# Turns by way of DRAM, one ring of eight weight buffers, and pauses counted in matmul time, in a two-layer mLSTM and RG-LRU trunk

## The chip, the cores and the metric

The kernel runs on one core of a Trainium2 chip. The metric is the device time of one execution in microseconds (us). A core has a matrix engine (PE, with its weight loads PEld), a vector engine (DVE), a scalar engine (ACT), GpSimd (POOL) and SyncE (SP, which only issues transfers), and 16 DMA engines that all queues share. Each engine runs its own list of instructions strictly in order; an instruction that waits holds up everything behind it on that engine.

## The reference

Two layers work on x (256 tokens by 2048 channels, float32); a final RMSNorm follows.

```
u = rms_norm(x, norm_g);  p = u @ w_in             # 12304 columns: q,k | v | o | z_a | gates | xb | z_b
q, k = silu(causal_dwconv(qk))                     # 4 taps, along the tokens
h = mlstm_chunkwise(q, k, v, i, log_f)             # 8 heads of matrix memory
y_a = head_norm(h * sigmoid(o)) * head_norm_g * silu(z_a)
xc = causal_dwconv(xb) + b
r, i = sigmoid(xc @ w_a + b_a), sigmoid(xc @ w_x + b_x)       # per head, 256 by 256
y_b = scan(a = exp(-8 r softplus(-lam)), xc * i * sqrt(1 - a*a)) * silu(z_b)
x = x + concat(y_a, y_b) @ w_out
```

## The kernel before, in words

**Products.** Every product is float32 made of three fp32r products: a weight is split into wH (a cast on ACT) and wL = w - wH (a subtraction on DVE), the activations likewise, and PE multiplies high by high, high by low and low by high. A "half" is the unit of work: 512 KB of weights (128 partitions by 1024 floats), its cast, its subtraction and 12 matmuls of 512 columns (24 shorter ones in a gate's half). `mm_a` (L392) keeps the tokens as rows of the result, `mm_b` (L412) the channels.

**Order.** `_sequence` (L45) writes out the order of the halves: per layer four groups of two heads and 512 channels, and in each group the columns for q/k, o, v, xb, z, z_b, the gates, and the 4 output chunks of the group before. Some products are made blockwise with seven instead of eight block products (`block_halves`, L1185): their weights are sums of blocks, which POOL makes ahead of time in DRAM tensors `w_d` with accumulating transfers (`weight_sums`, L1133), and each of their 84 pieces is a "block half" of 6 matmuls, set in between the others.

**The loop** (L1490) walks through the halves. Ahead of half n it loads (on SP), and prepares (wH, wL) halves up to three ahead (AHEAD, L28), for which there are four buffers (`wsp`, L125). Plain halves load into a ring of six buffers (`raw`, tag of the pool `wraw`, L123), block halves into two of their own (`rawb`, `wblk`, L124), with a rule for how far ahead of its place a block half is loaded (BLOCKS_AHEAD, L36 and L1495). Halves of q/k, xb and z_b are "paired": their 512 KB come from two units, in two transfers of 256 KB (L344).

**Work beside.** Everything else (convolution, gates, mLSTM) is written as generators that `pump` (L284) advances between the halves; a `yield "wait"` lets one pass go by, and `st["t"]` counts the matmul time laid down so far (2.72 us a half, 1.36 us a block half, L1520). `qk_post` (L706) makes the scores of the first head (`ps_S`, L752), pauses one pass (L762), makes those of the second, pauses three passes, and multiplies by v (`ps_n`, L675 to L677) for each head. The three auxiliary PSUM banks turn round among these, so the second head's second bank is free only when DVE has read the first head's first one (`Pt`, L758). What the builder lays down is then put into each engine's list by a scheduler of the language; it may move instructions of one engine past each other as long as data and ordering edges hold.

**Turns.** What needs channels as rows is turned: ACT writes `tok`, DVE transposes 32 by 32 blocks into `blk` (L528), and 16 transfers of 32 KB inside SBUF bring the blocks to their partitions, `fr` (L532): 8 from SP, 8 from POOL, and all 16 from SP for the last one, whose `back` is SP (L934). There are 35 turns. Readers of `fr` are `joined` (`ch`, L556), `split_channels` (`tok`, L548) and the z_b step (`zsg` and `zb`, L950 and L951). They are laid down LANDING = 10 us or FAR = 15 us of matmul time after the turn.

**The end.** The last item (`last_out`, L1325) has 16 halves: kp = 0 and 1 (four column chunks each) multiply y_a, kp = 2 and 3 multiply y_b for both token halves. The weights of kp = 2 are cast into buffers of their own, `w_own` (L1430), ordered behind the casts of y_b (`ybH`, `ybL`; L957 and L385); those of kp = 3 use the four `wsp` buffers, which the four halves of kp = 1 hold until PE has used them.

**Pace of the sums.** `weight_sums` keeps an account `st["dma"]` of transfer time: loads add COPY, accumulating transfers ADDING, turns TURN, and each half takes off its time times RATE (L1523). A sum is begun when the account is low, and each begins behind the cast then being made (`paced`, L276).

Of the kernel before, what the change touches and what calls it, by code (L numbers as in the profile page):

```python
# [9 lines left out]
F32 = mybir.dt.float32  # L10
# [6 lines left out]
P = 128  # L17
# [5 lines left out]
NG = 4  # L23
# [6 lines left out]
FAR = 15.0  # L30
BORDER = 7
BLANKS = 7
RATE = 0.9, 0.75
COPY, ADDING, TURN = 1.3, 2.6, 1.7
SUMS_FROM = 20
BLOCKS_AHEAD = 5  # L36
FULL = 3.0
LAG = {"wH": 0, "wL": 1}

# [60 lines left out]
def tile_trunk(ctx, tc, x, xt, par, gw, gb, ws, final_g, out):  # L100
    nc = tc.nc
    G, PE = nc.gpsimd, nc.tensor
# [17 lines left out]
    V, S = Behind(nc.vector, "wL"), Behind(nc.scalar, "wH")  # L120

    const = ctx.enter_context(tc.tile_pool(name="const", bufs=1))
    wraw = ctx.enter_context(tc.tile_pool(name="wraw", bufs=6))  # L123
    wblk = ctx.enter_context(tc.tile_pool(name="wblk", bufs=2))  # L124
    wsp = ctx.enter_context(tc.tile_pool(name="wsp", bufs=4))  # L125
    act = ctx.enter_context(tc.tile_pool(name="act", bufs=1))
    work = ctx.enter_context(tc.tile_pool(name="work", bufs=1))
# [1 line left out]
    dram = ctx.enter_context(tc.tile_pool(name="dram", bufs=1, space=bass.MemoryType.DRAM))  # L129
# [173 lines left out]
    def before(t):  # L303
        return st["t"] < t and not st.get("forced")

    def require(key):
        i = 0
        while key not in st:
            st["forced"] = True
            i = step(i)  # L310
        st["forced"] = False
# [16 lines left out]
    seq, blocks = _sequence(), _blocks()  # L328

    def load_half(hf):  # L330
        n = st["nload"]
        st["nload"] += 1
        (item, j), i = hf["at"], hf["i"]
        raw = hf["raw"] = wraw.tile([P, 1024], F32, tag="raw", name="raw")
        if n < 8:
            w = 512 if n < 2 else 1024
            load_xt(n // 2, i)
            for o in range(0, 1024, w):
                nc.sync.dma_start(out=raw[:, o : o + w], in_=ws[blocks[item, j]][:, 1024 * i + o : 1024 * i + o + w])
        elif hf["paired"]:  # L340
            o = 1024 * (j % 2) + 512 * i
            for s_ in range(2):
                u = blocks[item, 2 * s_ + j // 2]
                st["ld"] = nc.sync.dma_start(out=raw[:, 512 * s_ : 512 * s_ + 512], in_=ws[u][:, o : o + 512])  # L344
        else:
            st["ld"] = nc.sync.dma_start(out=raw, in_=ws[blocks[item, j]][:, 1024 * i : 1024 * i + 1024])
        st["dma"] += COPY
        if i == 1 and 3 <= n // 2 < 7:
            load_x(n // 2 - 3)

    def load_block(hf):
        if hf["made"]:
            require(hf["made"])
        raw = hf["raw"] = wblk.tile([P, 2, 512], F32, tag="rawb", name="rawb")
        st["ld"] = nc.sync.dma_start(out=raw.rearrange("p k n -> p (k n)"), in_=hf["from"])
        st["dma"] += COPY

    def add_unit(mms, before=None, after=None, paired=False, own=None):
        halves.append([dict(i=i, mm=mms[i], split=None, paired=paired, own=own and own[i],
# [2 lines left out]
    def prepare(hf):  # L362
        n = st["nprep"]
        if "from" not in hf:
            if hf["i"] == 0:
                if 3 <= n < 7:
                    use_x(n - 3)
            else:
                st["nprep"] += 1
        r = hf["raw"]  # L370
        if "from" not in hf:
            r = r.rearrange("p (s n) -> p s n", s=2)
        if hf["own"]:
            H, L = hf["own"]()
        else:
            H = wsp.tile([P, 2, 512], F32R, tag="H", name="wH")
            L = wsp.tile([P, 2, 512], F32R, tag="L", name="wL")
        opening = n < 4 and "from" not in hf
        for j, o in enumerate((slice(0, 1), slice(1, 2)) if opening else (slice(0, 2),)):
            if opening:  # L380
                kt = 4 * n + 2 * hf["i"] + j
                split_xT(0, kt // 4, xT_parts[n][:, kt % 4 : kt % 4 + 1, :], (kt,), st.get("wH"))
            st["wH"] = S.copy(out=H[:, o], in_=r[:, o])
            st["wL"] = tt_(L[:, o], r[:, o], H.bitcast(F32)[:, o], ALU.subtract)
            if hf["own"] and "ends" in st:  # L385
                order(st["wH"], st["ends"][0])
                order(st["wL"], st["ends"][1])
        if "loaded" in hf:
            st[hf["loaded"]] = True
        hf["split"] = (H.rearrange("p s n -> p (s n)"), L.rearrange("p s n -> p (s n)"))  # L390
# [129 lines left out]
    def swapped(tok, blk=None, back=G):  # L520


        if blk is None:
            blk = work.tile([P, 4, 256], F32, tag="blk", name="blk")
        fr = work.tile([P, 4, 4, 2, 32], F32, tag="fr", name="fr", bufs=2)
        st["lag"] += 1.2
        st["dma"] += TURN
        V.transpose(out=blk.rearrange("p m n -> p (m n)"), in_=tok.rearrange("p m c t j -> p (m c t j)"))  # L528
        for m in range(4):
            for a in range(4):  # L530
                engine = nc.sync if m < 2 else back
                i0 = engine.dma_start(out=fr[32 * m : 32 * m + 32, a].rearrange("p c t i -> p (c t i)"),  # L532
                                      in_=blk[32 * a : 32 * a + 32, m])
        if back is G:
            st["gq"] = i0
        return fr
# [152 lines left out]
    def v_post(l, g, acc):  # L689
        if g > 0:  # L690
            require(("lru", l, g - 1))
        vH = work.tile([P, 2, 2, 258], F32R, tag="sB", name="vH")
        vL = work.tile([P, 2, 2, 258], F32R, tag="sF", name="vL")
        require(("rstd", l))
        rstd = st["rstd", l]
        G.memset(vH.bitcast(F32)[:, :, :, 256:258], 1.0)
        G.memset(vL.bitcast(F32)[:, :, :, 256:258], 0.0)
        for t in range(2):
            av = acc[t].rearrange("p (h c) -> p h c", h=2)
            S.activation(out=vH[:, t, :, 0:256], in_=av, func=AF.Copy, scale=rstd[:, t : t + 1])  # L700
            stt(vL[:, t, :, 0:256], av, rstd[:, t : t + 1], vH.bitcast(F32)[:, t, :, 0:256], ALU.mult, ALU.subtract)
            st["lag"] += 0.75

        st["v", l, g] = (vH, vL)

    def qk_post(l, g, acc):  # L706
# [5 lines left out]
        def gen():  # L712
# [24 lines left out]
            tt_(q[:, :, 1, :], qc, q.bitcast(F32)[:, :, 0, :], ALU.subtract)  # L737
            st["turning"] = False
            yield 1.2
            for _ in range(3):  # L740
                yield "wait"
            while any((k, l, g) not in st for k in ("E", "v", "so")) or st["ch"]:
                yield "wait"
            st["ch"] = True
# [2 lines left out]
            for h in range(2):  # L747
# [11 lines left out]
                stt(Pt[:, h, :], Pt[:, h, :], DK_SCALE, E[:, h, :], ALU.mult, ALU.mult)  # L759
                yield 0.5  # L760
                if h == 0:
                    yield "wait"  # L762
            st["scores", l, g] = True
            PH = work.tile([P, 2, 384], F32R, tag="sD", name="PH")
            PL = work.tile([P, 2, 384], F32R, tag="sC", name="PL")
# [1 line left out]
            tt_(PL, Pt, PH.bitcast(F32), ALU.subtract)  # L767
            st["ch"] = False
            yield 1.0
            for _ in range(3):  # L770
                yield "wait"
            hh = work.tile([P, 2, 2, 256], F32, tag="sE", name="hh")
            mv = small.tile([P, 2, 2, 2], F32, tag="mv", name="mv", bufs=1)
            for h in range(2):
# [16 lines left out]
                    V.bn_aggr(out=mv[:, t, h, :], in_=bs)  # L791
                    yield 1.1
                if h == 0:
                    yield "wait"
            sd = small.tile([P, 2, 2], F32, tag="sd", name="sd", bufs=1)
            order(S.activation(out=sd, in_=mv[:, :, :, 1], func=AF.Sqrt, bias=epst), st["wH"])
            V.reciprocal(out=sd, in_=sd)
# [335 lines left out]
    def weight_sums():  # L1133
# [36 lines left out]
        while any(q for _, _, q in queues):  # L1170
            ready = [k for k in queues if k[2] and (k[2][0][0] is None or k[2][0][0] in st)]
            if not ready:
                yield "wait"
                continue
            l, p, q = ready[0]
            st["rate"] = RATE[l] if q[0][0] is None else 1.0
            while (st["dma"] > (COPY if q[0][0] is None else ADDING) or st["n"] - st.get("staged", -9) < 2) and not st.get("forced"):
                yield "wait"
            _, begin, made = q.popleft()
            begin()  # L1180
            if made:
                st[("made", l, p) + made] = True
            yield "wait"
# [285 lines left out]
    for l in reversed(range(DEPTH)):  # L1469
        for p in reversed(range(PRODUCTS[l])):  # L1470
# [8 lines left out]
            for i in reversed(range(len(parts))):  # L1479
                at = free[(i + 1) * (len(free) - 1) // len(parts)]  # L1480
                order_[at:at] = [parts[i]]
    plain_ = [hf for hf in order_ if "from" not in hf]
    blocks_ = [hf for hf in order_ if "from" in hf]
    count = 0
    for hf in order_:
        hf["at_n"] = count
        count += "from" not in hf

    nprep, nplain, nblock, lblock = 0, 0, 0, 0
    for n, hf in enumerate(order_):  # L1490
        st["n"] = n
        while nprep < len(order_) and nprep <= n + AHEAD:
            while st["nload"] < len(plain_) and st["nload"] <= nplain + 5:
                load_half(plain_[st["nload"]])
            while lblock < len(blocks_) and lblock <= nblock + 1 and nplain >= blocks_[lblock]["at_n"] - BLOCKS_AHEAD:  # L1495
                load_block(blocks_[lblock])
                lblock += 1
            st["behind"] = False
            prepare(order_[nprep])
            st["lag"] += 1.2  # L1500
            for key in done:
                done[key].append(st[key])
            st["behind"] = n >= 12
            if "from" in order_[nprep]:
                nblock += 1
            else:
                nplain += 1
            nprep += 1
        if hf["before"]:
            hf["before"]()  # L1510
# [108 lines left out]
```

## Time and profile before

| | |
|---|---|
| runs | 1479.97, 1482.12 and 1485.17 us, median 1482.12 |
| the profiled execution | 1480.39 us, of which the span from the first to the last instruction is 1478.7 |
| granted PE clock | 0.999 |
| busy | PE 1466.1 us, DVE 1168.8, ACT 970.2, POOL 251.3 |
| DMA | 386.23 MB, 261 GB/s in the mean; share of the 16 engines from 0.7 to 1.0 for most of the span |
| transfers of turns | 560 of 32 KB |

PE counts as busy while any matmul is in its pipeline, so the start-to-start distances of matmuls say more than its share: in the steady state 24 matmuls of 512 columns take 5.44 us. [...]

### The profile page before, as it was taken

How to read it: one execution, taken by the hardware profiler on the slowest of the kernel's cores; microseconds unless marked ns; L12 is line 12 of the kernel's file. 1: busy time of each engine (PE TensorE's matmuls, PEld its weight loads, DVE VectorE, ACT ScalarE, POOL GpSimd, SP SyncE). 2: the span in 40 equal slices, each digit the busy share in tenths (PEclk: the TensorE clock that was granted, in tenths of full speed). 3: DMA queues.
4: the chain of work that ended last, by engine and by line, in shares of the span. 5: the costliest groups of instructions: out<-in, count | busy, mean ns of one | idle time of the engine just before them, and what ended most of it. 6: DMA issues, size and time to landing. Idle time of an engine off the chain costs nothing.

```text
span 1478.7 us, 20749 instructions
## 1 busy us (share of the span) xinstructions
PE 1466.1 (99%) x6758; PEld 1222.1 (83%) x6758; DVE 1168.8 (79%) x1621; ACT 970.2 (66%) x1241; POOL 251.3 (17%) x468
## 2 busy tenths in 40 slices
PE   9999999999999999999999999999999999999997
PEld 7888888888888888888888888888888888888886
DVE  6798898887787776568857888988787876899775
ACT  6665766558665765548565667665577756776665
POOL 0131211101210131001221312110121101111012
PEclk9999999999999999999999999999999999999999
DMA  9889899989898788988788887999968889877874
GB/s 313 294 263 277 248 299 324 289 253 268 269 298 236 244 244 271 266 242 265 227 270 270 238 274 214 293 263 293 301 207 275 262 241 277 264 238 230 233 259 157
DMA packets 155533, 386.23 MB, mean 261 GB/s; under 512 B 23568, under 2 KB 35360, under 8 KB 155424
## 3 DMA queue, kind: packets, MB, share of 16 engines
q1 hardware_dynamic: 128864, 315.91, 62.6%
q0 software_dynamic: 24096, 64.53, 21.4%
q10 hardware_dynamic: 2464, 4.47, 0.8%
q8 instruction: 53, 0.87, 0.2%
q14 instruction: 56, 0.46, 0.1%
HBM read 347.57 MB, written 58.74 MB: 275 GB/s over the span
## 4 chain that ended last, share of the span: by engine, by line
PE 81%; DMA 8%; DVE 5%; ACT 2%; SPq 2%; issue 2%; POOL 0%; DVEq 0%; ACTq 0%
PE acc L409 68%; DMA raw<-in_ws_dram 5%; PE ps_b L1232 3%; PE ps_b L1233 3%; PE ps_b L1234 3%; PE ps_gt L878 2%; DVE wL L114 2%; SPq L532 1%; DMA xp<-in_xt_dram 1%; DMA x_d<-x_acc 1%; DMA fr<-blk 1%; ACT wH L114 1%; DMA x_acc<-in_x_dram 1%; DVE scs L114 1%; PE ps_n L677 0%
## 5 line engine op out<-in xcount | busy, mean ns | idle before, releaser
L409 PE MATMUL acc<-wH,x_s 128*128 128x512 f32 x2624 | 821.7, 389 | 0.2 <-ACT wH L114 0.2
L114 DVE TENSOR_TENSOR wL<-raw,wH 128x1024 fp32r<-128x1024 f32 (+1 forms) x484 | 578.8, 1200 | 201.3 <-ACT wH L114 199.2
L114 ACT CAST wH<-raw 128x1024 fp32r<-128x1024 f32 (+1 forms) x484 | 499.1, 1037 | 326.0 <-PE acc L409 237.7
L409 PEld LDWEIGHTS acc<-wH,x_s 128*128 128x128 f32 x2624 | 492.4, 188 | 102.3 <-ACT wH L114 0.8
L409 PE MATMUL acc<-wL,x_s 128*128 128x512 f32 x1312 | 509.5, 389 | 0.0
L409 PEld LDWEIGHTS acc<-wL,x_s 128*128 128x128 f32 x1312 | 246.3, 188 | 51.3 <-DVE wL L114 0.7
L532 POOL DMA_DIRECT2D fr<-blk x256 | 126.8, 506 | 357.8 <-DVE blk L114 188.6
L114 DVE TENSOR_TENSOR wL<-rawb,wH 128x1024 fp32r<-128x1024 f32 x84 | 102.4, 1219 | 26.8 <-ACT wH L114 26.8
L114 ACT CAST wH<-rawb 128x1024 fp32r<-128x1024 f32 x84 | 88.3, 1051 | 52.6 <-PE acc L409 35.2
L1140 POOL DMA_DIRECT2D w_d<-in_ws_dram x72 | 53.7, 746 | 381.7 <-ACT wH L114 333.4
L114 ACT ACT_TABLE_LOAD x62 | 79.5, 1283 | 13.3 <-DVE qc L114 3.1
L409 PE MATMUL acc<-wH,ybL 128*128 128x512 f32 x224 | 87.4, 390 | 0.3 <-DVE ybL L988 0.3
L409 PE MATMUL acc<-wH,ybH 128*128 128x512 f32 x224 | 87.4, 390 | 0.0
L409 PE MATMUL acc<-wH,yaH 128*128 128x512 f32 x224 | 87.4, 390 | 0.0
L409 PE MATMUL acc<-wL,ybH 128*128 128x512 f32 x224 | 87.2, 389 | 0.0
L409 PE MATMUL acc<-wH,yaL 128*128 128x512 f32 x224 | 87.2, 389 | 0.0
L409 PE MATMUL acc<-wL,yaH 128*128 128x512 f32 x224 | 87.2, 389 | 0.0
L1028 POOL DMA_DIRECT2D x_d<-stage x24 | 21.1, 880 | 221.7 <-ACT stage L114 186.9
L409 PEld LDWEIGHTS acc<-wH,ybL 128*128 128x128 f32 x224 | 42.1, 188 | 9.8 <-DVE ybL L988 1.0
L409 PEld LDWEIGHTS acc<-wH,yaL 128*128 128x128 f32 x224 | 42.0, 188 | 8.8
L409 PEld LDWEIGHTS acc<-wH,ybH 128*128 128x128 f32 x224 | 42.0, 188 | 8.7 <-ACT ybH L987 0.3
L409 PEld LDWEIGHTS acc<-wH,yaH 128*128 128x128 f32 x224 | 42.1, 188 | 8.6
(231 smaller groups left out, 1767.2 us busy)
## 6 DMA issues: line engine op xcount, KB each, us to landing
raw<-in_ws_dram SPq DMA_DIRECT2D x294, 512.0 KB, 6.7
raw<-in_ws_dram SPq DMA_DIRECT2D x372, 256.0 KB, 5.9
w_d<-in_ws_dram POOLq DMA_DIRECT2D x72, 512.0 KB, 8.7
rawb<-w_d SPq DMA_DIRECT2D x48, 512.0 KB, 6.2
rawb<-in_ws_dram SPq DMA_DIRECT2D x36, 512.0 KB, 7.5
x_d<-stage POOLq DMA_DIRECT2D x24, 512.0 KB, 7.0
fr<-blk SPq DMA_DIRECT2D x272, 32.0 KB, 3.3
fr<-blk POOLq DMA_DIRECT2D x256, 32.0 KB, 3.5
```

Source lines behind the costliest of these rows:

```text
L114: ins = f(*a, **k)
L409: st["mm"] = PE.matmul(o, a_[:, kt, P * t : P * t + P], W[:, k], start=b, stop=z)
L532: i0 = engine.dma_start(out=fr[32 * m : 32 * m + 32, a].rearrange("p c t i -> p (c t i)"), in_=blk[32 * a : 32 * a + 32, m])
L878: PE.matmul(o, W[:, ib, jl], xs[:, ib, a, :], start=j == 0 and i == 0 and W is Hv and a == 0, stop=i == 1 and W is Lv, skip_group_check=True)
L1028: st["gq"] = G.dma_start(out=xd[c], in_=stage, accum_op=ALU.add)
L1140: i0 = G.dma_start(out=wd[l][p][to][j][:, cs], in_=(wd[l][p][src][j] if src == 0 else block_unit(l, p, *src, j))[:, cs], **how)
L1232: PE.matmul(box["b"], aH, Hv[:, k], start=opening and k == 0, stop=False, skip_group_check=True)
L1233: PE.matmul(box["b"], aH, Lv[:, k], start=False, stop=False, skip_group_check=True)
L1234: PE.matmul(box["b"], aL, Hv[:, k], start=False, stop=kp == 3 and k == 1, skip_group_check=True)
```

## The change

- **Ring.** One pool of eight buffers (SLOTS) takes plain and block halves in the order of their use; a load is issued as soon as eight are not out. The separate pool and its rule are gone, and `load_block` is part of `load_half`.
- **Paired halves** come in one transfer of 512 KB with rows of 2 KB.
- **Turns.** Four transfers of 128 KB on SP write `blk` into a DRAM tile `moved` (two of them take turns), and one transfer of 512 KB reads it back as `fr`, issued by `back`: POOL, or SP for the last turn. The read waits until the four writes have landed. The bytes of a turn are moved twice.
- **Pauses.** In groups 0 to 2 the pauses in `qk_post` last until a given matmul time has been laid down: 7.0, 4.0, 7.0 and 2.7 us in place of 3, 1, 3 and 1 passes; group 3 keeps the passes.
- **Constants.** RATE 1.0 and 0.8 in place of 0.9 and 0.75, TURN 2.9 in place of 1.7. `weight_sums` looks anew for the first ready sum after each wait.
- **Memsets** of the ones and zeros beside v go from POOL to DVE.

```diff
-RATE = 0.9, 0.75
-COPY, ADDING, TURN = 1.3, 2.6, 1.7
+RATE = 1.0, 0.8
+COPY, ADDING, TURN = 1.3, 2.6, 2.9
+SLOTS = 8
-BLOCKS_AHEAD = 5
...
-    wraw = ctx.enter_context(tc.tile_pool(name="wraw", bufs=6))
-    wblk = ctx.enter_context(tc.tile_pool(name="wblk", bufs=2))
+    wraw = ctx.enter_context(tc.tile_pool(name="wraw", bufs=SLOTS))
...
+    def pause(g, us, waits):
+        t = st["t"] + us
+        while before(t) if g < NG - 1 else waits > 0:
+            waits -= 1
+            yield "wait"
...
-            for s_ in range(2):
-                u = blocks[item, 2 * s_ + j // 2]
-                st["ld"] = nc.sync.dma_start(out=raw[:, 512 * s_ : 512 * s_ + 512], in_=ws[u][:, o : o + 512])
+            o, u = 1024 * (j % 2) + 512 * i, blocks[item, j // 2]
+            st["ld"] = nc.sync.dma_start(out=raw.rearrange("p (s n) -> p s n", s=2),
+                                         in_=ws[u : u + 3 : 2, :, o : o + 512].rearrange("s p n -> p s n"))
...
-        for m in range(4):
-            for a in range(4):
-                engine = nc.sync if m < 2 else back
-                i0 = engine.dma_start(out=fr[32 * m : 32 * m + 32, a].rearrange("p c t i -> p (c t i)"),
-                                      in_=blk[32 * a : 32 * a + 32, m])
+        moved = dram.tile([P, 4, 256], F32, tag="moved", name="moved", bufs=2)
+        for a in range(4):
+            nc.sync.dma_start(out=moved[:, a].rearrange("(m j) n -> j m n", m=4), in_=blk[32 * a : 32 * a + 32])
+        i0 = back.dma_start(out=fr.rearrange("p a c t i -> p a (c t i)"), in_=moved)
...
-        G.memset(vH.bitcast(F32)[:, :, :, 256:258], 1.0)
-        G.memset(vL.bitcast(F32)[:, :, :, 256:258], 0.0)
+        V.memset(vH.bitcast(F32)[:, :, :, 256:258], 1.0)
+        V.memset(vL.bitcast(F32)[:, :, :, 256:258], 0.0)
...
-            for _ in range(3):
-                yield "wait"
+            yield from pause(g, 7.0, 3)
...
                 if h == 0:
-                    yield "wait"
+                    yield from pause(g, 4.0, 1)
...
-            while st["nload"] < len(plain_) and st["nload"] <= nplain + 5:
-                load_half(plain_[st["nload"]])
-            while lblock < len(blocks_) and lblock <= nblock + 1 and nplain >= blocks_[lblock]["at_n"] - BLOCKS_AHEAD:
-                load_block(blocks_[lblock])
-                lblock += 1
+            while st["nload"] < min(len(order_), nprep + SLOTS):
+                load_half(order_[st["nload"]])
```

The halves and their order stay as they are, and so does every matmul. Three places in the engines' lists follow.

ACT's list around the scores of layer 0, group 2, before: `stage` is the evacuation of an output chunk, the first two `Pt` belong to the first head, the others to the second.

```order
L114 CAST wH<-raw 128x1024 x2
L114 COPY stage<-acc 128x1024
L114 COPY Pt<-ps_S 128x256
L114 COPY Pt<-ps_S 128x128
L114 CAST wH<-raw 128x1024 x2
L114 COPY Pt<-ps_S 128x256
L114 COPY Pt<-ps_S 128x128
```

The same place in the changed kernel:

```order
L114 CAST wH<-raw 128x1024 x2
L114 COPY stage<-acc 128x1024
L114 COPY Pt<-ps_S 128x256
L114 COPY Pt<-ps_S 128x128
L114 CAST wH<-raw 128x1024 x3
L114 COPY Pt<-ps_S 128x256
L114 COPY Pt<-ps_S 128x128
```

One more cast stands between the heads here, and on PE two halves (24 matmuls of 512 columns) in place of one between the first head's scores and the second's.

ACT's list near the end, before: `tok` fills the last turn, `zsg` reads its `fr`, and the casts ahead of `zsg` run from kp = 0's last to kp = 1's last.

```order
L114 ACTIVATE tok<-acc,rstd 128x4x4x32 x2
L114 CAST wH<-raw 128x1024 x5
L114 ACT_TABLE_LOAD
L114 ACTIVATE zsg<-fr 128x1024
L114 CAST ybH<-zb 128x512 x2
L114 CAST w_own<-raw 128x1024 x4
L114 CAST wH<-raw 128x1024 x4
```

The same stretch in the changed kernel:

```order
L114 ACTIVATE tok<-acc,rstd 128x4x4x32 x2
L114 CAST wH<-raw 128x1024 x6
L114 ACT_TABLE_LOAD
L114 ACTIVATE zsg<-fr 128x1024
L114 CAST wH<-raw 128x1024 x2
L114 CAST ybH<-zb 128x512 x2
L114 CAST w_own<-raw 128x1024 x4
L114 CAST wH<-raw 128x1024
```

Three of the four casts for kp = 3 now stand ahead of `ybH` and `w_own`; on DVE the `wL` that belong to them likewise stand ahead of `ybL`.

SP's list at the same place, before:

```order
L346 DMA raw<-in_ws_dram 128x1024 x4
L532 DMA fr<-blk 32x256 x16
L346 DMA raw<-in_ws_dram 128x1024 x7
L1400 DMA out_dram<-x_acc 128x512 x7
L1615 UNCONDITIONAL_BRANCH
```

and in the changed kernel:

```order
L356 DMA raw<-in_ws_dram 128x1024 x4
L531 DMA moved<-blk 32x4x256 x4
L356 DMA raw<-in_ws_dram 128x1024 x2
L532 DMA fr<-moved 128x1024
L356 DMA raw<-in_ws_dram 128x1024 x3
L1399 DMA out_dram<-x_acc 128x512 x7
```

Two weight loads now stand between the writes of the last turn and its read, and three behind it.

More of the change, by code (lines that the diff above doesn't have):

```diff
@@ L332, in load_half @@
         st["nload"] += 1
+        if "from" in hf and hf["made"]:
+            require(hf["made"])
+        raw = hf["raw"] = wraw.tile([P, 1024], F32, tag="raw", name="raw")
+        st["dma"] += COPY
+        if "from" in hf:
+            st["ld"] = nc.sync.dma_start(out=raw, in_=hf["from"])
+            return
         (item, j), i = hf["at"], hf["i"]
-        raw = hf["raw"] = wraw.tile([P, 1024], F32, tag="raw", name="raw")
         if n < 8:
@@ L340, in load_half @@
         elif hf["paired"]:
-            o = 1024 * (j % 2) + 512 * i
-            for s_ in range(2):
-                u = blocks[item, 2 * s_ + j // 2]
-                st["ld"] = nc.sync.dma_start(out=raw[:, 512 * s_ : 512 * s_ + 512], in_=ws[u][:, o : o + 512])
+            o, u = 1024 * (j % 2) + 512 * i, blocks[item, j // 2]
+            st["ld"] = nc.sync.dma_start(out=raw.rearrange("p (s n) -> p s n", s=2),
+                                         in_=ws[u : u + 3 : 2, :, o : o + 512].rearrange("s p n -> p s n"))
         else:
             st["ld"] = nc.sync.dma_start(out=raw, in_=ws[blocks[item, j]][:, 1024 * i : 1024 * i + 1024])
-        st["dma"] += COPY
         if i == 1 and 3 <= n // 2 < 7:
             load_x(n // 2 - 3)
[L351 to L356, printed above, removed]
     def add_unit(mms, before=None, after=None, paired=False, own=None):
@@ L369, in prepare @@
                 st["nprep"] += 1
-        r = hf["raw"]
-        if "from" not in hf:
-            r = r.rearrange("p (s n) -> p s n", s=2)
+        r = hf["raw"].rearrange("p (s n) -> p s n", s=2)
         if hf["own"]:
@@ L769, in gen @@
             yield 1.0
-            for _ in range(3):
-                yield "wait"
+            yield from pause(g, 7.0, 3)
             hh = work.tile([P, 2, 2, 256], F32, tag="sE", name="hh")
@@ L793, in gen @@
                 if h == 0:
-                    yield "wait"
+                    yield from pause(g, 2.7, 1)
             sd = small.tile([P, 2, 2], F32, tag="sd", name="sd", bufs=1)
@@ L1176, in weight_sums @@
             st["rate"] = RATE[l] if q[0][0] is None else 1.0
-            while (st["dma"] > (COPY if q[0][0] is None else ADDING) or st["n"] - st.get("staged", -9) < 2) and not st.get("forced"):
+            full = st["dma"] > (COPY if q[0][0] is None else ADDING) or st["n"] - st.get("staged", -9) < 2
+            if full and not st.get("forced"):
                 yield "wait"
+                continue
             _, begin, made = q.popleft()
@@ L1481, in tile_trunk @@
                 order_[at:at] = [parts[i]]
[L1482 to L1489, printed above, removed]
+    nprep = 0
     for n, hf in enumerate(order_):
@@ L1503, in tile_trunk @@
             st["behind"] = n >= 12
[L1504 to L1507, printed above, removed]
             nprep += 1
```

## Prediction

> **What bounds the kernel now.** I read the page's busy shares first, then PE's waits, the chain that ended last, the timeline around each PE wait, and last the landing times of transfers and the windows.
>
> ```profile
> span 1478.7 us, 20749 instructions
> PE 1466.1 (99%) x6758; PEld 1222.1 (83%) x6758; DVE 1168.8 (79%) x1621; ACT 970.2 (66%) x1241; POOL 251.3 (17%) x468
> ...
> 181.40 5.44 PE acc L409 x24
> ```
>
> PE is the bound. The chain's row shows the steady state: 24 matmuls in 5.44 us, 227 ns each, so 2.72 us for a half of 12. The change leaves every matmul and their order alone, so it can win only what PE waits, and lose by making PE wait more.
>
> ```profile
> PE ps_S L752 <- DVE Pt L114: 2.1, 2, 1.9
> PE ps_blank L147 <- DVE blank L114: 1.3, 1, 1.3
> PE ps_rb L480 <- DVE dg L114: 0.5, 1, 0.5
> PE acc L409 <- DVE ybL L988: 0.3, 1, 0.3
> ```
>
> PE's waits (total, times, longest) come to 4.2 us in these rows. 1.3 of it is the start of the program. So the ceiling of any gain is near 3 us, 0.2% of the span. The profiled execution took 1480.4 us, its span plus 1.7. I sum against it. The two middle ones of the four executions known are 1480.4 and 1482.1, whose mean, 1481.3, is 0.9 above the profiled one; the forecast adds that. About 0.3%, 4.4 us, is what a measurement of this kernel can tell from no change; so "faster" is below 1476.8 and "slower" above 1485.7, both around 1481.3.
>
> **Pauses.** PE's rows, then ACT's, around the largest wait, and PE's second one:
>
> ```profile
> 439.38 0.27 PE L754 MATMUL ps_S<-qks 128*128 128x256 f32 x1
> 439.49 0.28 PE L752 MATMUL ps_S<-qks 128*128 128x256 f32 x1
> ...
> 442.70 0.27 PE L754 MATMUL ps_S<-qks 128*128 128x256 f32 x1
> 444.88 0.39 PE L752 MATMUL ps_S<-qks 128*128 128x256 f32 x1 [1.91 <-DVE Pt L114]
> ...
> 844.51 0.39 PE L752 MATMUL ps_S<-qks 128*128 128x256 f32 x1 [0.16 <-DVE Pt L114]
> ```
>
> ```profile
> 443.09 1.01 ACT L114 COPY stage<-acc 128x1024 f32<-128x1024 f32 x1 [5.31 <-PE ps_S L754]
> ```
>
> The first head's scores pass from L754 to L752 in 0.11 us; the second's took 2.18, so 2.07 are lost, 0.16 more than the wait in brackets. ACT had evacuated `stage` before it could copy `Pt`, and the bank was free only after that. In the changed lists two halves of PE work stand there instead of one, 2.7 us more for the bank to come free. That exceeds 2.07, so this wait goes. The second wait (0.16, with the same 0.16 of refill 0.3) gets the same extra half. What is late next at both places is nothing that the lists show. **−2.1 − 0.3 = −2.4 us**, between −2.4 and 0.
>
> **Turns.** A turn was 8 issues on SP beside 8 on POOL; now it is four writes on SP, a wait for them, and one read. Rows: SP's issues of `fr`, the ACT reader, then one turn at 1128 us and the cast two casts behind its reader.
>
> ```profile
> L532 SPq DMA_DIRECT2D fr<-blk x272: 507/588/1564, 63.1 to 1440.3; - x136
> L114 ACT COPY ch<-fr x16: 1035/1050/1055, 71.0 to 1356.8; 128x1024 f32<-128x1024 f32 x16
> ```
>
> ```profile
> 1128.31 5.70 SPq L532 DMA_DIRECT2D fr<-blk  x8
> ```
>
> ```profile
> 1136.59 1.04 ACT L114 COPY ch<-fr 128x1024 f32<-128x1024 f32 x1
> ...
> 1139.34 1.06 ACT L114 CAST wH<-raw 128x1024 fp32r<-128x1024 f32 x1
> ```
>
> The transfer rows (KB each, median us from issue to landing):
>
> ```profile
> w_d<-in_ws_dram POOLq DMA_DIRECT2D x72, 512.0 KB, 8.7
> rawb<-w_d SPq DMA_DIRECT2D x48, 512.0 KB, 6.2
> ...
> fr<-blk SPq DMA_DIRECT2D x272, 32.0 KB, 3.3
> ...
> x_d<-x_acc ACTq DMA_DIRECT2D x8, 512.0 KB, 6.4
> ...
> nb<-nG_d POOLq DMA_DIRECT2D x8, 256.0 KB, 7.3
> ```
>
> The fourth write is issued 3 × 0.59 = 1.8 us after the first. It lands after 3.3 us (the 32 KB row) to 6.4 (512 KB into DRAM); on the line between them 128 KB give 3.9. The read lands after 6.2 to 8.7 us; I take 7.3, the row nearest the middle, a read from DRAM on POOL's queue. A turn so takes 1.8 + 3.9 + 7.3 = **13.0 us, bounds 11.3 and 16.9**. The old one's last issue alone came some 5 us after the first.
>
> Is that covered? At 1128 us the reader `ch` ran 8.3 us after the first issue. In the changed list of ACT two more casts stand ahead of most `ch`; here that is the end of the cast at 1139.34, 1140.4, so 12.1 us after the issue. A turn of 13.0 makes ACT wait 0.9 there. Queued behind it on ACT are the casts, behind those DVE's `wL`, then PE. Their cover in the same stretch:
>
> ```profile
> 1132.54 1.05 ACT L114 CAST wH<-rawb 128x1024 fp32r<-128x1024 f32 x1 [1.67 <-PE acc L409]
> ```
>
> ```profile
> 1133.62 1.23 DVE L114 TENSOR_TENSOR wL<-rawb,wH 128x1024 fp32r<-128x1024 f32 x1 [0.58 <-ACT wH L114]
> ```
>
> ```profile
> 1139.36 0.39 PE L1233 MATMUL ps_b<-wL,x_s 128*128 128x512 f32 x1
> ```
>
> `wL` is done at 1134.85 and PE wants it at 1139.36: 4.5 us to spare. So a turn reaches PE only from 12.1 + 4.5 = 16.6 us on, where the cover is ordinary. Where it is thin I put **+0.6 us** in all for the 35 turns, bounds 0 and 0.3 × 16 readers = 4.8 (16.9 less 16.6).
>
> The Trainium skill, page "DMA: Bandwidth & Descriptors", section "Anatomy of one DMA — SWDGE (gpsimd) path", gives a transfer some 2.0 us fixed plus its bytes at 436 GB/s, and lays most of the fixed part to the receipt of the write, heaviest where the target is HBM. By it, as an estimate, a turn would take 1.8 + 2.3 + 3.2 = 7.3 us, add no wait, and the whole sum below would be 0.6 + 0.5 us lower. The trace disagrees in size: 512 KB take 6.2 to 8.7 us here, where the queues are shared, and the 6.4 of the write into DRAM does not stand above the reads.
>
> POOL loses eight issues a turn and gains one; SP loses four or more. Nobody on PE's path waits for these issues in the rows above, so that is worth 0.
>
> **Sums and bytes.** 35 turns × 0.52 MB, once more, are 18.4 MB on 386. RATE lets the sums run ahead faster: in POOL's list the fifth turn has 16 of the 72 `w_d` transfers ahead of it, 11 before. The windows (the last three columns are PE's clock, DMA share and GB/s):
>
> ```profile
> 75.00:100.00 25.00, 25.00 (x111) 20.32 (x110) 24.47 (x53) 15.76 (x19) 7.33 (x12) 1.00 0.85 271
> 125.00:150.00 25.00, 25.00 (x129) 21.36 (x128) 20.04 (x39) 16.03 (x21) 6.29 (x12) 1.00 0.91 282
> 200.00:250.00 50.00, 50.00 (x222) 41.39 (x222) 44.03 (x52) 35.25 (x40) 6.31 (x11) 1.00 1.00 328
> ```
>
> One more sum (0.52 MB read and written) and one turn's extra 0.52 MB in 25 us add 63 GB/s: 334 and 345, above the 328 at which a window with a share of 1.00 still kept PE busy for 50.00 of 50. The excess, 17 GB/s for 25 us, is 0.4 MB or 1.3 us of transfer. Eight buffers of 2.72 us each hold 21.8 us of weights against 6 to 9 us of landing; that hides it. **0**, bounds 0 and +4 (three such windows in a row, the ring empty).
>
> **Ring, pairing, memsets.** The ring issues the same bytes of weights; no PE wait in the rows ends on a load, so 0 (−0.5 to +0.5 at the head, where eight loads are issued in place of six). The memsets go to DVE, where the nearest small operation and its slack are these:
>
> ```profile
> 1132.04 1.00 DVE L114 TENSOR_SCALAR E<-nb,at 128x256 f32<-128x256 f32 x4
> ```
>
> ```profile
> DVE wL L114 <- ACT wH L114: 226.0, 176, 4.5
> ```
>
> 16 of them at 0.25 us are 4 us, spread out, on an engine that waits 226 us for casts: 0. Without that cover, 4.
>
> **The end.** ACT, DVE, SP and PE around the last turn, before:
>
> ```profile
> 1437.53 1.05 ACT L114 CAST wH<-raw 128x1024 fp32r<-128x1024 f32 x1 [1.67 <-PE acc_x L1355]
> 1441.62 1.28 ACT L114 ACT_TABLE_LOAD   x1 [3.04 <-DMA fr<-blk]
> 1442.92 1.06 ACT L114 ACTIVATE zsg<-fr 128x1024 f32<-128x1024 f32 x1
> 1445.27 1.15 ACT L114 CAST ybH<-zb 128x512 fp32r<-128x512 f32 x2 [1.29 <-DVE zb L114]
> ```
>
> ```profile
> 1445.92 1.29 DVE L114 TENSOR_TENSOR ybL<-zb,ybH 128x512 fp32r<-128x512 f32 x2 [0.69 <-ACT ybH L114]
> 1447.39 2.36 DVE L114 TENSOR_TENSOR w_own<-raw,w_own 128x1024 fp32r<-128x1024 f32 x2 [0.18 <-ACT w_own L114]
> ```
>
> ```profile
> 1429.90 11.02 SPq L532 DMA_DIRECT2D fr<-blk  x16
> ```
>
> ```profile
> 1445.49 0.39 PE L1353 MATMUL acc_x<-wH,yaH 128*128 128x512 f32 x1
> ...
> 1448.67 0.50 PE L1354 MATMUL acc<-w_own,ybH 128*128 128x512 f32 x1
> ```
>
> PE starts kp = 1's last half at 1445.49, and its first `w_own` product with the low weights at 1448.67, 0.1 after DVE made them (1447.39 + 1.18). There is no spare time. In the changed list the casts of kp = 3's first three halves, and their `wL`, stand ahead of `ybH`, `ybL` and `w_own`; the third can start only when PE has left the buffer of kp = 1's third half, at 1445.49 and 0.2 (as 1437.53 follows the half's end at 1445.49 − 3 × 2.72 = 1437.33). That is 1445.7 at the soonest. The turn sets the other limit: 1429.90 + 13.0 = 1442.9 for `fr`, table load and `zsg` 2.36, one cast 0.95: 1446.2. Then cast 0.95, `ybH` 1.15: 1448.3; on DVE `wL` until 1448.5, `ybL` 1.29, `w_own` 1.2: 1451.0; PE at 1451.1, against 1448.67. **+2.4 us**, of which 0.5 is the turn and 1.9 the order alone. From an arrival at 1442.4 each us later costs a us: bounds 0 (the order is cheaper than I read it) and +6.3 (16.9 us for the turn).
>
> **The sum.** −2.4 + 2.4 + 0.6 + 0 + 0 = +0.6 us on 1480.4: 1481.0. With the 0.9: **1481.9 us**. The gain of the pauses is given back at the end.
>
> **The rivals.**
> 1. The end costs nothing: PE's buffers and `fr` come early enough and DVE takes `ybL` without a hitch. −2.4 + 0.6 on 1481.3: 1479.5, within the bound. For it: last landing before, 1441.6, came 1.3 us after the last issue at 1440.3, so transfers are quick there. Against: 1445.7 for the third cast doesn't depend on the transfers. Chance 0.13.
> 2. Every wait goes: 4.2 us and the 0.3 of refill, 1476.8, just at "faster". Against: the wait at the start and the one at L480 aren't touched. Chance 0.06.
> 3. The turns are late: landing at the upper end, 16.9, which decides from 16.6 us at the readers and from 1442.4 at the end. +4.8 and +6.3 − 2.4 = +8.7: 1490.0. For it: landing at 8.7 is the median of 72 transfers on the same queue. Against: the 3.3 row. Chance 0.14.
> 4. The sums crowd the loads: share 1.00 in the windows from 75 to 150, the ring runs empty, +4 on the forecast: 1485.9. Against: 1.00 was covered at 200 to 250. Chance 0.07.
> 5. That the change doesn't do what it says: the pauses leave the scores' place in the list as it is. The lists show otherwise; no chance.
>
> The forecast keeps 0.60. Faster 0.06, same 0.60 + 0.13 = 0.73, slower 0.21. The range: from 1478.0, between the first two rivals, to 1488.5, short of the third: at most 0.06 below, some 0.10 above.
>
> **What would show it.** Right: no `ps_S` row above 0.5 us among PE's waits; a PE wait of about 2.4 us at the first `w_own` products, released by ACT or DVE; `fr<-moved` landing at 6 to 9 us, writes at 3 to 6; PE's sum of waits 4 to 6 us. Wrong: a `ps_S` wait that stays; waits of PE for `wH` or `wL` right behind `ch` (turns); SP's weight loads landing above 9 us with PE waiting for `raw`'s casts between 75 and 150 us (sums); a span below 1475.

## The result, and the profile after

The changed kernel takes 1493.68 us (median of 7 runs, 1490.42 to 1498.08) beside 1482.84 for the kernel before: ratio 1.0075, 95% interval 1.006 to 1.0091. It is slower by 11 us. That lies outside the range of the prediction; the nearest thing in it is the third rival, the late turns at 1490.0. The execution that was profiled took 1497.1 us. The page, and PE's waits:

```profile
span 1495.4 us, 19493 instructions
...
PE 1471.5 (98%) x6758; PEld 1223.8 (82%) x6758; DVE 1166.4 (78%) x1637; ACT 969.6 (65%) x1242; POOL 133.7 (9%) x214
```

```profile
PE acc L409 <- DVE wL L114: 9.6, 6, 2.8
PE acc L409 <- ACT wH L114: 1.9, 1, 1.9
PE ps_blank L146 <- DVE blank L114: 1.3, 1, 1.3
PE acc L1352 <- ACT w_own L114: 0.9, 2, 0.5
PE ps_S L750 <- DVE Pt L114: 0.8, 1, 0.8
PE acc_x L1352 <- ACT w_own L114: 0.5, 1, 0.5
PE acc L409 <- DVE ybL L985: 0.3, 1, 0.3
```

PE's waits sum to 15.3 us, 10.9 more than the 4.4 before. PE's busy time rose by 5.4 us (1471.5 less 1466.1) for the same matmuls. The two make 16.3 of the 16.7 us by which the span grew. The wait that leads now, `wL` with 9.6 us, is not among the rows before. Both `ps_S` waits of before are gone; the one of 0.8 us is new and stands at 1195 us, just behind the late turn at 1188. Set beside the kernel before, matmul by matmul, the delay comes in a few steps: behind turns at 179, 414, 445, 567 to 612 and 1188 us, at 845 us behind another transfer, and at the end.

**A late turn.** The largest one: its transfers, the reader `ch` on ACT, what follows on DVE, and PE.

```profile
425.22 2.31 SPq L531 DMA_DIRECT2D moved<-blk  x4
427.63 6.50 SPq L356 DMA_DIRECT2D raw<-in_ws_dram  x5
```

```profile
432.72 0.56 POOL L532 DMA_DIRECT2D fr<-moved  x1 [17.85 <-DMA moved<-blk]
```

```profile
433.26 1.05 ACT L114 CAST wH<-raw 128x1024 fp32r<-128x1024 f32 x1 [0.75 <-PE acc L409]
440.68 1.05 ACT L114 COPY ch<-fr 128x1024 f32<-128x1024 f32 x1 [6.36 <-DMA fr<-moved]
441.76 2.08 ACT L114 ACTIVATE xc<-ch,pars 128x256 f32<-128x256 f32 x4
443.75 1.98 ACT L114 CAST wH<-raw 128x1024 fp32r<-128x1024 f32 x2
```

```profile
434.35 1.22 DVE L114 TENSOR_TENSOR wL<-raw,wH 128x1024 fp32r<-128x1024 f32 x1 [0.58 <-ACT wH L114]
442.39 4.55 DVE L114 SCALAR_TENSOR_TENSOR xc<-ch,pars,xc 128x255 f32<-128x255 f32 x11 [6.83 <-ACT xc L114]
446.86 1.22 DVE L114 TENSOR_TENSOR wL<-raw,wH 128x1024 fp32r<-128x1024 f32 x1
```

```profile
448.14 0.50 PE L409 MATMUL acc<-wL,yaH 128*128 128x512 f32 x1 [2.80 <-DVE wL L114]
```

The writes go out at 425.2, the read is issued at 432.7 and lands at 440.7: 15.5 us. ACT had come to `ch` at 434.3, 9.1 us after the writes. No cast runs for the 6.4 us of the wait. Then the convolution that reads `ch`, eleven operations of 4.55 us together, stands ahead of the next `wL` on DVE: that subtraction follows 12.5 us after the one before it, and PE waits 2.8. ACT's waits for `ch` over the whole program, after and before:

```profile
ACT ch L114 <- DMA fr<-moved: 28.3, 7, 6.4
```

```profile
ACT ch L114 <- DMA fr<-blk: 6.9, 3, 3.1
```

ACT's waits for the two other readers, `zsg` and `tok`, are 8.2 and 4.0 us after the change.

**PE at half speed.** PE's granted clock (third from the right) in two windows around that stall:

```profile
440.00:444.80 4.80, 4.71 (x23) 3.59 (x21) 2.37 (x6) 4.09 (x7) 0.00 (x0) 1.00 0.80 231
...
449.70:452.00 2.30, 2.30 (x7) 1.77 (x6) 2.19 (x5) 1.59 (x2) 0.00 (x0) 0.50 1.00 239
```

Ahead of the stall the clock is 1.00. From 1.4 us after its end (449.53) it is 0.50 for 3.41 us, and a matmul of 512 columns takes 0.43 us in place of 0.23. 13 such matmuls, here and at 849 us, cost 2.6 us; the kernel before had none. The Trainium skill, page "TensorE: Matmul & The Clock Gate", section "Part 1: The HAM clock gate (the "warmup" mystery)", says that the clock falls to half after an idle window of some 3.4 us, and that the window runs free of the program. The trace agrees that the window runs free: the two slow phases last 3.41 us each and begin at 449.53 and 848.89 us, 117 times 3.413 us apart. On the length it differs, and the measurement decides: in the 3.41 us ahead of each phase PE had stood still for only 2.0 and 2.3 us. The stall of 2.2 us at 414 us fell into two such windows, 0.9 and 1.4 us, and no slow phase followed.

**The step at 845 us** is no turn. POOL and DVE there, then PE:

```profile
831.28 0.52 POOL L625 DMA_DIRECT2D nG_d<-scs  x1 [3.44 <-DVE scs L114]
833.17 0.84 POOL L1137 DMA_DIRECT2D w_d<-in_ws_dram  x1 [1.38 <-ACT wH L114]
834.67 0.58 POOL L653 DMA_DIRECT2D nb<-nG_d  x1 [0.66 <-DMA nG_d<-scs]
```

```profile
842.56 1.01 DVE L114 TENSOR_SCALAR E<-nb,at 128x256 f32<-128x256 f32 x4 [3.94 <-DMA nb<-nG_d]
```

```profile
846.82 0.49 PE L409 MATMUL acc<-wH,x_s 128*128 128x512 f32 x1 [1.86 <-ACT wH L114]
848.27 0.50 PE L409 MATMUL acc<-wL,x_s 128*128 128x512 f32 x1 [0.95 <-DVE wL L114]
```

A sum (`w_d`) stands between the two small transfers of the gates, and `nb` lands 7.8 us after its issue at 834.7. Before, nothing stood between them, and `nb` took 4.7:

```profile
824.27 0.53 POOL L626 DMA_DIRECT2D nG_d<-scs  x1 [5.87 <-DVE scs L114]
826.77 0.60 POOL L654 DMA_DIRECT2D nb<-nG_d  x1 [1.97 <-DMA nG_d<-scs]
```

ACT's list also changed there:

```profile
834.16 1.05 ACT L114 CAST wH<-raw 128x1024 fp32r<-128x1024 f32 x1 [1.29 <-issue]
837.56 1.28 ACT L114 ACT_TABLE_LOAD   x1 [2.34 <-DVE qc L114]
...
843.60 0.85 ACT L114 ACTIVATE E<-E 128x768 f32<-128x768 f32 x1 [2.38 <-DVE E L114]
844.77 1.04 ACT L114 CAST qks<-qc 128x1024 fp32r<-128x1024 f32 x1 [0.33 <-DVE qc L114]
845.73 1.99 ACT L114 CAST wH<-raw 128x1024 fp32r<-128x1024 f32 x2
```

Between the casts at 834.2 and 845.7 there is none, 11.6 us. Before, two more stood there, one ahead of `E` and one behind `qsg`.

**The end** went nearly as forecast. ACT, then PE's waits on `w_own`:

```profile
1460.33 1.05 ACT L114 CAST wH<-raw 128x1024 fp32r<-128x1024 f32 x1 [0.23 <-PE acc_x L1354]
1461.28 1.14 ACT L114 CAST ybH<-zb 128x512 fp32r<-128x512 f32 x2
1462.33 3.89 ACT L114 CAST w_own<-raw 128x1024 fp32r<-128x1024 f32 x4
```

```profile
1463.43 0.50 PE L1352 MATMUL acc<-w_own,ybH 128*128 128x512 f32 x1 [0.47 <-ACT w_own L114]
1464.37 0.49 PE L1352 MATMUL acc<-w_own,ybH 128*128 128x512 f32 x1 [0.44 <-ACT w_own L114]
1465.32 0.50 PE L1352 MATMUL acc_x<-w_own,ybH 128*128 128x512 f32 x1 [0.45 <-ACT w_own L114]
```

The third cast of kp = 3 starts 0.23 us after PE has left its buffer, `ybH` and `w_own` follow, and PE loses 1.9 us more here than before (2.4 forecast). That is the forecast's 1.9 for the order alone. Its other 0.5, for the turn, did not come: the cast waited for PE and not for the turn, which took 12.9 us.

### The profile page after: what moved, and what is told of

Same layout as the page of the kernel before. It is cut to its first block, busy times and chain, and to the rows that moved or that the text cites. A ratio compares the mean times of both kernels' runs of the same rounds, so it can differ in the third digit from the quotient of the medians.

```text
span 1495.4 us, 19493 instructions
## 1 busy us (share of the span) xinstructions
PE 1471.5 (98%) x6758; PEld 1223.8 (82%) x6758; DVE 1166.4 (78%) x1637; ACT 969.6 (65%) x1242; POOL 133.7 (9%) x214
## 4 chain that ended last, share of the span: by engine, by line
PE 73%; DMA 9%; issue 8%; DVE 6%; ACT 3%; SPq 1%; POOL 0%; POOLq 0%; DVEq 0%; ACTq 0%
PE acc L409 59%; DMA fr<-moved 5%; PE ps_gt L875 3%; DMA moved<-blk 2%; DVE wL L114 2%; PE ps_b L1231 2%; PE ps_b L1233 2%; PE ps_b L1232 2%; DVE xc L114 1%; DMA raw<-in_ws_dram 1%; DVE qc L114 1%; ACT wH L114 1%; DVE blk L114 1%; SPq L531 1%; PE acc L1354 1%
## 5 line engine op out<-in xcount | busy, mean ns | idle before, releaser
L114 DVE TENSOR_TENSOR wL<-raw,wH 128x1024 fp32r<-128x1024 f32 (+1 forms) x568 | 678.9, 1203 | 228.5 <-ACT wH L114 222.4
L114 ACT CAST wH<-raw 128x1024 fp32r<-128x1024 f32 (+1 forms) x568 | 584.5, 1038 | 364.1 <-PE acc L409 286.3
L532 POOL DMA_DIRECT2D fr<-moved x34 | 19.3, 567 | 481.5 <-DMA moved<-blk 438.1
L114 DVE SCALAR_TENSOR_TENSOR xc<-ch,pars,xc 128x255 f32<-128x255 f32 (+2 forms) x96 | 42.3, 477 | 16.6 <-ACT xc L114 16.4
L409 PEld LDWEIGHTS acc<-wL,yaH 128*128 128x128 f32 x224 | 42.2, 189 | 12.2 <-DVE wL L114 3.6
L409 PEld LDWEIGHTS acc<-wL,ybH 128*128 128x128 f32 x224 | 42.1, 188 | 10.6 <-DVE wL L114 2.2
```

What stands on the lines that cost most here:

```text
L114: ins = f(*a, **k)
L409: st["mm"] = PE.matmul(o, a_[:, kt, P * t : P * t + P], W[:, k], start=b, stop=z)
L532: i0 = back.dma_start(out=fr.rearrange("p a c t i -> p a (c t i)"), in_=moved)
```

## The experiments

Two theories. **The late turn:** the readers of `fr` that wait stand 9 to 13 us behind the turn in ACT's list, turns by way of DRAM take 10 to 17, and what stands behind the reader takes the rest. **Contention:** more bytes, sums that run ahead and the ring's deeper queue make all transfers late. A third cause, sums that come too late, is seen in the traces of three runs. All ratios are to the kernel before, with 95% intervals, from 5 rounds. The steps named at places in the program come from each kernel's profiled execution, set matmul by matmul beside the one before.

**One part alone: the pauses, on the kernel before.**

```diff
-            for _ in range(3):
-                yield "wait"
+            yield from pause(g, 7.0, 3)
```

(and so at the other three places.)

> The kernel before with the pauses in PE time alone. The prediction's term: both waits for ps_S go, 2.4 us, 1480.4 us beside 1482.8. Rival, the later scores bunch with other work on ACT and DVE, as after the changed kernel's stall at 1194 us: 1483 or more.

1480.60 us, ratio 0.9985 (0.9975 to 0.9995). No `ps_S` wait is left:

```profile
PE ps_blank L147 <- DVE blank L114: 1.3, 1, 1.3
PE ps_rb L486 <- DVE dg L114: 1.1, 1, 1.1
PE acc L1358 <- DVE w_own L114: 0.8, 1, 0.8
...
```

By the medians the term stands, 2.2 us for the 2.4 forecast, with an interval of 0.7 to 3.7. The two profiled executions don't show it in their total (1480.62 us beside 1480.39): there the `ps_S` waits go, and the waits for `dg` and `w_own` above grow.

**Later readers, the same transfers.**

```diff
-LANDING = 10.0
-FAR = 15.0
+LANDING = 16.0
+FAR = 21.0
```

> The changed kernel with LANDING 16 and FAR 21 in place of 10 and 15; the transfers and their bytes stay. Theory of the late turn: the readers stand some 6 us later, beyond the landing, so most of the 12 us of stalls go: 1484 to 1487 us. Rival, contention by more bytes or by sums running ahead: nothing changes, 1493 us. Against both: later readers push the work behind them (scores, sums) together, and other waits appear.

1483.63 us, ratio 1.0001 (0.999 to 1.0012): 10 us of the loss are back, with every byte still moved twice and RATE as changed. Turns take a median of 12.7 us there (13.5 in the changed kernel), with a longest of 17.9. ACT's waits for them:

```profile
ACT ch L114 <- DMA fr<-moved: 2.6, 4, 1.0
```

2.6 us in place of 28.3. What is left are the steps at 834 us (5.4) and at the end (3.4, of which 1.4 are at half clock). Halfway, with LANDING 13 and FAR 18:

> The changed kernel with LANDING 13, FAR 18, halfway. Late readers, turns of 10 to 17 us: between 1493.7 and 1483.6, some 1487 us, the stalls behind turns of over 15 us left. If what helped was the other order that the scheduler made, and no matter of the landing: 1483 or 1493, no value between.

1485.84 us, ratio 1.0023 (1.001 to 1.0036), a value between, as the late turn has it, though its interval just touches that of LANDING 16. ACT's waits for `ch` are between too: 9.5 us, beside 28.3 and 2.6.

**The way through DRAM on the kernel before**, with TURN 2.9 and the old RATE:

> The kernel before with the turns by way of DRAM alone, and TURN 2.9. Theory of the late turn: stalls behind the readers as in the changed kernel, 8 to 12 us over before: 1491 to 1495 us. Rival, ring, RATE or pauses carry the loss: within 2 us of before, 1481 to 1485.

1511.55 us, ratio 1.0192 (1.0161 to 1.0223), more than either theory said. Its longest stall begins in SP's list, and SP's waits say why:

```profile
1281.89 6.86 SPq L344 DMA_DIRECT2D raw<-in_ws_dram  x4
1288.85 0.44 SPq L531 DMA_DIRECT2D moved<-blk  x1
1296.61 0.33 SPq L355 DMA_DIRECT2D rawb<-w_d  x1
1296.99 1.43 SPq L531 DMA_DIRECT2D moved<-blk  x3
```

```profile
SPq L355 <- DMA w_d<-in_ws_dram: 27.2, 4, 8.9
```

```profile
1319.00 0.80 PE L1231 MATMUL ps_b<-wH,sums 128*128 128x512 f32 x1 [8.02 <-ACT wH L114]
```

The load of a sum (`rawb<-w_d`) stands between the first and the second write, and is issued 7.8 us after the first: it waits for the sum itself, which lands at 1296.60. The writes behind it wait, and the turn takes 22.6 us. The next sum stands behind the turn's read in POOL's list and lands at 1313.99; the load that needs it goes out at 1314.01, its cast follows, and PE waits 8.0. Neither theory named this, and the kernel before and the changed kernel have no such wait of SP. By the program's account the constants do it: with TURN 2.9 each turn loads the account more, the old RATE takes no more off, and the sums fall behind. The 70th of POOL's 76 transfers into `w_d` is issued at 1248 us here, at 1039 in the kernel before, and at 1050 in the changed kernel, whose RATE is higher. So this run does not test the way through DRAM alone; none has it with TURN 1.7. With later readers as well (LANDING 16, FAR 21):

> The kernel before with the turns by way of DRAM, and LANDING 16, FAR 21. Late readers as the whole cause of its 28.7 us: near 1485 us. Without the ring the writes also stand behind loads on SP that wait for buffers (the 8.4 us at 1311 us, the 2.8 at 322): then 1492 to 1500 us.

1500.12 us, ratio 1.0123 (1.0102 to 1.0143). Later readers bring 11 us here too, and the two stalls at 835 and 1297 us, 4.6 and 8.4 us, stay. Neither is a late turn. At 835 us a sum holds up the gates' small transfers (below). At 1297 PE waits for the cast of a block half whose sum lands at 1299.94, and SP issues its load at 1299.96; SP waited 15.3 us for sums in all. With their slow phases the two steps cost 6.4 and 13.8 us, and the profiled span is 19.4 us above that of the kernel before: taken off, they leave the way through DRAM with later readers no cost there.

**The turns of before in the changed kernel** (16 transfers inside SBUF, TURN 1.7):

> The changed kernel with the turns of before: 16 transfers inside SBUF, TURN 1.7. Theory of the late turn (a turn by way of DRAM lands 13.9 to 17.3 us after blk, its reader stands 9 to 12 us behind it in ACT's list, and the casts queue behind the reader): the stalls at 179, 414, 445, 567, 612, 718 and 1188 us go, some 12 us, so about 1482 us if the 5 us at 845 us (late nb) and the 2.2 us at the end stay, 1477 if the late nb goes too. Rival, the sums and the ring crowd the DMA engines: the 18 MB less help by 1 to 3 us only, about 1491. Rival, the order that the scheduler makes of ring and pauses: 1492 or more.

1491.52 us, ratio 1.0049 (1.0033 to 1.0065), far less back than the late turn said. With TURN 1.7 at the new RATE the sums run further ahead than in the changed kernel: the 53rd transfer into `w_d` is issued at 579 us, at 667 there, and at 801 in the kernel before. The step at 845 us went (no sum stands between the two small transfers here); those at 445 and 1188 went; a stall at 408 us came, and the end lost 6.6 in place of 1.9. SP and ACT at 408 us:

```profile
393.52 8.38 SPq L532 DMA_DIRECT2D fr<-blk  x8
```

```profile
408.48 1.04 ACT L114 COPY ch<-fr 128x1024 f32<-128x1024 f32 x1 [6.58 <-DMA raw<-in_ws_dram]
```

SP needs 8.4 us for the 8 small issues, and `ch` waits 6.6. The releaser named is a load; the landing of the last small transfer is missing from the trace, so that it was that transfer is inferred. This looks like contention, and RATE tells: with RATE 0.9 and 0.75 besides,

> The changed kernel with the turns of before inside SBUF and with RATE as before: ring, pauses and memsets are left. Sums that crowd the queues: the stalls of the run with SBUF turns at 180 and 408 us, 1.9 and 6 us, go, 1483 to 1485 us, the 6.6 us at the end staying. Ring as their cause (one queue of SP runs further ahead, so a turn's transfers queue behind more loads): they stay, 1490.

1484.26 us, ratio 1.0006 (0.9992 to 1.0019): the stalls at 180 and 408 us are gone, and the end keeps its 5.7. The old RATE alone in the changed kernel:

> The changed kernel with RATE 0.9 and 0.75 as before. In POOL's list no sum stands between the two transfers nG_d and nb of layer 1 now. Theory (sums pulled forward delay nb): the 5 us at 845 us go; and if the crowding by sums is what makes the turns land at 14 to 17 us, more goes: 1480 to 1484 us. Theory of the late turn without crowding: only the 5 us, 1488 to 1489. If the nb stall is the order of ACT's list alone, 1493.

1496.93 us, ratio 1.0102 (1.0078 to 1.0125), a miss for each theory. The step at 845 us fell from some 5 to 2.2, but TURN 2.9 with the old RATE makes the sums late here too (the 70th transfer at 1232 us): SP waits 35.4 us for them, the writes of a turn at 1276 us are issued 7.4 us after `blk`, a cast waits 7.2 us for a sum's load, and a step of 9.5 us at 1296 came. So the old RATE brought a loss of its own. It did not make the turns quick: their median is 13.3 us beside 13.5, and ACT waits 23.1 us for `ch`. So the faster pace of the sums is not what makes the turns by way of DRAM late.

**The read in four pieces**, each behind its own write:

```diff
-        i0 = back.dma_start(out=fr.rearrange("p a c t i -> p a (c t i)"), in_=moved)
+        for a in range(4):
+            i0 = back.dma_start(out=fr[:, a].rearrange("p c t i -> p (c t i)"), in_=moved[:, a])
```

> The changed kernel with the read of a turn in four, each behind its own write. Late turn as a chain of two whole landings: the reads overlap the writes, the turn is 1 to 2 us shorter, 2 to 6 us of the stalls go, 1488 to 1491 us. Late turn by queueing behind weights and sums, which four reads share as one does: 1493.

1508.21 us, ratio 1.0187 (1.0166 to 1.0209), a miss: the turn's median is 13.3 us, hardly shorter. Each piece of 128 KB lands 5.9 us after its issue, where the whole 512 KB took 6.8, so cutting it saves little; why the whole is slower still was not settled.

**Mended.** The changed kernel with LANDING 16 and FAR 21, no sum laid down between the gates and `nb`, and the casts of kp = 3 ordered behind those of y_b:

```diff
-            if hf["own"] and "ends" in st:
+            if (hf["own"] or hf.get("late")) and "ends" in st:
...
-            if full and not st.get("forced"):
+            if (full or st.get("hold")) and not st.get("forced"):
```

(`late` is set for kp = 3; `hold` from the start of `gates_gen` to the issue of the first `nb`.)

> The changed kernel with LANDING 16 and FAR 21, no new sum begun between the gates and nb, and the casts of kp = 3 ordered behind those of y_b. Each term by itself: 5.4 us at 835 us and 3.3 us at the end go, 1475 us. If the nb stall is the order of ACT's list alone, it stays and 1480 is reached; if the end only waits for the last turn instead, 1478.

1477.22 us, ratio 0.9964 (0.995 to 0.9978): faster than both kernels. The step at 834 us is 1.0 and the end loses nothing. PE's waits and POOL's list:

```profile
PE acc L409 <- DVE wL L114: 1.4, 2, 0.7
PE ps_blank L146 <- DVE blank L114: 1.3, 1, 1.3
...
```

```profile
819.73 0.53 POOL L626 DMA_DIRECT2D nG_d<-scs  x1 [3.11 <-DVE scs L114]
823.70 0.58 POOL L654 DMA_DIRECT2D nb<-nG_d  x1 [3.44 <-DMA nG_d<-scs]
```

The same with the turns inside SBUF:

> The fastest kernel so far (LANDING 16, FAR 21, both orders mended) with the turns inside SBUF again. If the way through DRAM itself gains nothing, and the gain is from pauses, ring and the two orders: 1476 to 1478 us, as with DRAM. If the DRAM way pays once its readers stand late enough (fewer issues on SP and POOL, no small packets among the loads): 1480 or more here, with loads that come late.

1479.74 us, ratio 0.9981 (0.9968 to 0.9993). The intervals overlap, so which way is better there stays open. And ring, pauses and both orders with SBUF turns, the old RATE and the old distances:

> Ring, pauses and memsets with the turns of before, RATE of before, no sum begun between the gates and nb, and the casts of kp = 3 behind those of y_b. The term of the end by itself: 5.7 us less than without that order (1484.3), 1478 to 1479 us. If the last turn's 16 issues on SP set the end there, little of it comes back: 1482 or more.

1482.44 us, ratio 0.999 (0.9977 to 1.0003). The end gave back 4.2 of its 5.7 us; but the scheduler put another sum between the two small transfers in spite of `hold`, and a step of 4.6 us at 834 came back. In the four other kernels with a sum between them, the changed one, the two with later readers alone and the one with the read in pieces, the step is 3.3 to 6.1 us; in the five kernels of the ring without one it is 0 to 2.2. In the two kernels of before with the DRAM way a sum stands directly ahead of `nG_d`, which then took some 7 us, and the step is 7.4 and 6.4 us. So the step comes and goes with a sum next to the small transfers, and it grows with the time from the issue of `nG_d` to the landing of `nb`: 8.0 and 8.3 us where there is no step, 9.0 to 9.2 where it is some 1 us, 10.4 where it is 2.2, 10.9 to 11.7 where it is 3.3 (without a slow phase of PE) to 6.1 (with one), 13.0 and 14.0 where it is 6.4 and 7.4. That points to the landing; a run with ACT's other order alone was not made.

## Why the prediction was wrong

- **The step that failed** is "So a turn reaches PE only from 12.1 + 4.5 = 16.6 us on, where the cover is ordinary. Where it is thin I put +0.6 us in all". The duration was right in the middle: 13.0 forecast, a median of 13.5 and a span of 9.9 to 17.3 measured. (The sum lacked one term, the time from the last landing of the writes to the issue of the read. In the 17 turns whose landings the trace has, it is 0.5 to 1.1 us, and 2.6 to 3.3 in three where the read stands behind other work of POOL, the longest turn among them.) The distance and the cover were wrong. Both were read at one quiet place (1128 us), and ACT had come to the readers behind which PE stalled 9.1 to 13.2 us after the turn's first write. The 4.5 us of cover held for the casts behind the reader, but the reader's own followers stand ahead of `wL` on DVE (4.55 us at 442.4). The steps behind late turns cost 13.9 us (1.2, 2.6, 5.0, 2.1 and 3.0, slow phases with them) instead of 0.6, and the kernel with later readers takes 10 back.
- **A median isn't what decides.** The sum used the middle of the turn's range for 35 turns; PE was held by turns above it, of 13.8 to 17.3 us. Rival 3 lies nearest in time, but by luck: it priced only what exceeded 16.6 us, 0.3 us for each of 16 readers, and 6.3 at the end; in truth ACT waited 28.3 us for `ch` in 7 waits, and the end cost less than forecast.
- **The clock** had no term; 2.6 us.
- **The sums** had 0, with an empty ring as the bound. The ring did not run empty; the sum that came to stand between `nG_d` and `nb` cost some 5 us.
- **The ring, pairing and memsets** had 0, with 0.5 either way at the head. The first 130 us became 2.0 us shorter, of which PE's early wait at L480 is 0.5. All ten kernels with these three parts have 1.4 to 2.3 us there, the three on the old loop none; which part brings it was not tested.
- **Right:** the pauses (2.2 measured alone, 2.4 forecast) and the order at the end (1.9 measured, of the 2.4 forecast with the turn; nothing once the order is mended).

Summed from the profiled executions: late turns 13.9, the place at 845 us 4.7, the end 1.9, less 2.4 for the pauses and 2.0 won in the first 130 us, give 16.1 of the 16.7 us between them. The medians lie 11 us apart, since the changed kernel's profiled execution was 3.4 us above its median and the first 2.5 below.

## What to carry to other kernels

Where an engine works its list in order, a slower transfer is weighed at every one of its readers: how long after the issue the engine really reaches the reader, and all that stands between the reader and the bound engine's food, on the other engines too. Where the distances are constants of the program, a change of the transfer is half a change; moving the readers with it turned 1.0075 into 1.0001 here, and two orders mended beside it made 0.9964. Where a constant stands for a transfer's cost in an account, it and the rate that pays it off belong together: the new TURN with the old RATE put the sums some 200 us behind and PE's food with them. And where a scheduler decides, one transfer let in ahead of a small one that others wait for cost 4.7 us here, twice what the pauses gained.

## What the runs showed of the hardware

- PE at half clock: in every trace all phases at a clock of 0.50 begin on one grid of 3.41 us, whose offset from the start of the program differs from trace to trace. Those in mid-program last 3.41 us or a whole multiple, up to 13.65. Of these 21, 19 follow a window of the grid in which PE had stood still for 1.84 us or more (1.84 to 3.41), and two, near the end, a window of 1.31. One window of 1.91 us was not followed by one, nor any of 1.80 or less but those two. So of stalls of much the same length some have a phase and some don't: one of 2.25 us between the starts of two matmuls, at 844 us in the changed kernel, fell for the greater part, with a shorter one behind it, into one window (2.3 us idle) and had one; 2.63 at 414 us there, and 2.23 at 833 us with LANDING 13, lay across two and had none. Every stall of 2.8 us or more had one. A stall so cost up to some 2.4 us more than its length (12 matmuls at 0.43 us in place of 0.23, behind the one at 408 us with SBUF turns).
- A piece of a quarter of the bytes is hardly quicker: 128 KB reads in pieces landed after 5.9 us, 512 KB after 6.8, on the same queue.
- A 512 KB write and read through DRAM, as four writes and one read, took 10 to 17 us from the first issue; 16 transfers of 32 KB inside SBUF had a median of 7.6 in the kernel before, and up to 14, counted to the last landing in the trace, where one of the 16 is missing.
